# Row-wise sum of squared differences on one core: larger and uneven pieces at the end, a late piece of y, squares in place on ACT

One core of a Trainium2 chip. The metric is the device time of one execution in microseconds (us), the median of the fast runs; lower is better. The kernel is bounded by its input stream (DMA engines busy for 93.8% of the span), so a change of a few tenths of a microsecond is what there is to win, and each reading below is of that size.

## The reference

```python
batch, dim = 1024, 4096          # x and y are float32, standard normal
def reference(x, y, axis):       # axis = -1
    return np.sum((x - y) ** 2, axis=axis).astype(np.float32)
```

Two inputs of 16.8 MB each go in, 4 KB come out. Each partition holds 8 rows of 4096 columns, one after the other, so a partition reads 32768 contiguous columns of x and as many of y.

## The kernel before

Rows 0 to 3 of x and y come in one load each, rows 4 and 5 in one load each, rows 6 and 7 in eight pairs of loads that shrink towards the end. X and Y hold six rows, and rows 6 and 7 take the place of rows 0 and 1. DVE subtracts in place, ACT squares with a sum along the row, DVE squares a few small pieces itself, and the last square on DVE starts from the sum of all earlier parts of row 7 (`head`).

```python
H = 6
X = nc.alloc_sbuf_tensor("X", [P, H * D], F32).ap()
Y = nc.alloc_sbuf_tensor("Y", [P, H * D], F32).ap()
junk = nc.alloc_psum_tensor("junk", [P, D], F32).ap()

w6 = [3328, 768]
w7 = [1280, 1024, 640, 512, 320, 320]
squares = "ADAAAADD"                     # A: on ACT, D: on DVE
# ... cut ...
def square_on_act(c0, w, acc):
    h0 = c0 % (H * D)
    nc.scalar.wait_ge(diffs, n["diffs"])
    if n["acts"]:
        nc.scalar.wait_ge(acts, n["acts"])      # junk is written by all of them
    nc.scalar.activation(
        out=junk[:, 0:w], in_=X[:, h0 : h0 + w], func=Square, accum_out=acc
    ).then_inc(acts, 1)
# ... cut: rows 0 to 5; the loads of rows 6 and 7 are issued after two squares ...
for k, w in enumerate(w6 + w7):
    k7 = k - len(w6)
    if k7 == K - 1:
        add_up(head, part7)              # ahead of the last subtraction
    nc.vector.wait_ge(loaded[2 + k], 32)
    # ... cut ...
    sub(c0, w)
    # ... cut: square on ACT or DVE, the last one on DVE from head ...
```

Of the kernel before, what the change touches and what calls it, by code (L numbers as in the profile page):

```python
# [1 line left out]
_os.environ.setdefault("NEURON_RT_ULTRASERVER_MODE", "4")  # L2

# [3 lines left out]


class Program:






    def __init__(self, nc, tc):
        self.nc, self.hook = nc, tc.instruction_hook
        self.here = nc.cur_bb.bb.instructions
        self.entry = nc.main_func.blocks[0].instructions
        nc.remove_inst_callback(self.hook)  # L20
        self.lower, nc._always_lower_symbolic_ap = nc._always_lower_symbolic_ap, False
        self.before = len(self.here)

    def _take(self):
        taken = self.here[self.before :]
        del self.here[self.before :]
        return taken

    def _put(self, where):
        self.entry[where:where] = self._take()  # L30

    def early(self, engine):

        self._put(
            next(
                n
                for n, i in enumerate(self.entry)
                if i.engine == engine and str(i.opcode) == "Drain"
            )
        )  # L40

    def close(self):

        self._put(
            next(
                n for n, i in enumerate(self.entry) if str(i.opcode) == "UnconditionalBranch"
            )
        )
        self.nc._always_lower_symbolic_ap = self.lower
        self.nc.push_inst_callback(self.hook)  # L50


def kernel(tc, x, y, axis, out):
    nc = tc.nc
    P = nc.NUM_PARTITIONS
    F32 = mybir.dt.float32
    Square = mybir.ActivationFunctionType.Square
    mult, add = mybir.AluOpType.mult, mybir.AluOpType.add

    B, D = x.shape  # L60
    R = B // P


    xv = x.rearrange("(p r) d -> p (r d)", p=P)
    yv = y.rearrange("(p r) d -> p (r d)", p=P)
    ov = out.rearrange("(p r) -> p r", p=P)


    H = 6
    X = nc.alloc_sbuf_tensor("X", [P, H * D], F32).ap()  # L70
    Y = nc.alloc_sbuf_tensor("Y", [P, H * D], F32).ap()
    results = nc.alloc_sbuf_tensor("results", [P, R], F32).ap()
    junk = nc.alloc_psum_tensor("junk", [P, D], F32).ap()

    w6 = [3328, 768]
    w7 = [1280, 1024, 640, 512, 320, 320]
    squares = "ADAAAADD"
    assert sum(w6) == sum(w7) == D
    K = len(w7)
    part6 = nc.alloc_sbuf_tensor("part6", [P, len(w6)], F32).ap()  # L80
    part7 = nc.alloc_sbuf_tensor("part7", [P, K - 1], F32).ap()
    head = nc.alloc_sbuf_tensor("head", [P, 1], F32).ap()

    diffs = tc.alloc_semaphore("diffs")
    acts = tc.alloc_semaphore("acts")
    sums = tc.alloc_semaphore("sums")
    stored = tc.alloc_semaphore("stored")
    n = dict(diffs=0, acts=0, sums=0)

    prog = Program(nc, tc)  # L90

    def load(sem, src, dst, c0, c1):
        h0 = c0 % (H * D)
        nc.sync.dma_start(out=dst[:, h0 : h0 + c1 - c0], in_=src[:, c0:c1]).then_inc(sem, 16)  # L94

    loaded = []

    def load_pair(c0, c1):
        sem = tc.alloc_semaphore("loaded%d" % len(loaded))
        load(sem, xv, X, c0, c1)  # L100
        load(sem, yv, Y, c0, c1)
        loaded.append(sem)


    load_pair(0, 4 * D)
    prog.early(mybir.EngineType.SP)
    load_pair(4 * D, 6 * D)


    def sub(c0, w):  # L110
        h0 = c0 % (H * D)
        a = X[:, h0 : h0 + w]
        nc.vector.tensor_sub(out=a, in0=a, in1=Y[:, h0 : h0 + w]).then_inc(diffs, 1)  # L113
        n["diffs"] += 1

    def square_on_act(c0, w, acc):
        h0 = c0 % (H * D)
        nc.scalar.wait_ge(diffs, n["diffs"])
        if n["acts"]:
            nc.scalar.wait_ge(acts, n["acts"])  # L120
        nc.scalar.activation(  # L121
            out=junk[:, 0:w], in_=X[:, h0 : h0 + w], func=Square, accum_out=acc
        ).then_inc(acts, 1)
        n["acts"] += 1

    def square_on_dve(c0, w, acc, start):
        h0 = c0 % (H * D)
        nc.vector.wait_ge(diffs, n["diffs"])
        nc.vector.tensor_tensor_reduce(  # L129
            out=Y[:, h0 : h0 + w],  # L130
            in0=X[:, h0 : h0 + w],
            in1=X[:, h0 : h0 + w],
            scale=1.0,
            scalar=start,
            op0=mult,
            op1=add,
            accum_out=acc,
        ).then_inc(sums, 1)
        n["sums"] += 1

    def add_up(acc, parts, after=None):
        nc.vector.wait_ge(acts, n["acts"] if after is None else after)
        nc.vector.wait_ge(sums, n["sums"])  # L143
        nc.vector.tensor_reduce(  # L144
            out=acc, in_=parts, axis=mybir.AxisListType.X, op=add
        ).then_inc(sums, 1)
        n["sums"] += 1

    for r in range(6):
        if r in (0, 4):  # L150
            nc.vector.wait_ge(loaded[r // 4], 32)
        sub(r * D, D)
        square_on_act(r * D, D, results[:, r : r + 1])
        if r == 1:

            nc.sync.wait_ge(acts, 2)
            c0 = 6 * D
            for w in w6 + w7:
                load_pair(c0, c0 + w)
                c0 += w  # L160

    c0 = 6 * D
    for k, w in enumerate(w6 + w7):
        k7 = k - len(w6)
        if k7 == K - 1:
            add_up(head, part7)
        nc.vector.wait_ge(loaded[2 + k], 32)
        if k7 == K - 1:
            nc.vector.wait_ge(sums, n["sums"])  # L169
        sub(c0, w)  # L170
        if k7 < 0:
            acc = part6[:, k : k + 1]
        elif k7 < K - 1:
            acc = part7[:, k7 : k7 + 1]
        if k7 == K - 1:
            square_on_dve(c0, w, results[:, 7:8], head)
        elif squares[k] == "A":
            square_on_act(c0, w, acc)
        else:
            square_on_dve(c0, w, acc, 0.0)  # L180
        if k7 == 2:
            add_up(results[:, 6:7], part6, after=acts6)
        if k7 == -1:
            acts6 = n["acts"]
        c0 += w

    nc.sync.wait_ge(sums, n["sums"])
    nc.sync.wait_ge(acts, n["acts"])
    nc.sync.dma_start(out=ov, in_=results).then_inc(stored, 16)
    nc.sync.wait_ge(stored, 16)  # L190
    prog.close()


# [1 line left out]
_INS = ['x', 'y', 'axis']  # L195
_OUTS = [((1024,), 'float32')]

_NUMBERS = {'axis': -1}


# [26 lines left out]
```

## Time and profile before

| | before |
|---|---|
| time, median of 3 | 86.75 us |
| span of the profiled execution | 85.2 us |
| DVE busy / ACT busy | 38.0 us (45%) / 30.7 us (36%) |
| DMA engines busy | 93.8% of the span |
| last y piece landed | 81.2 |
| output store issued | 82.91 |

The page and the views behind it are shown in the prediction. In timeline lines the first number is the start in us, the second the duration; the bracket says how long the engine had been idle and what ended that. A landing is the start of a load's issue plus the time "to landing" of the list of DMA issues; that list gives it to 0.1 us, so a distance between two landings is good to about 0.1.

The profiled execution itself took 87.03 us, 0.28 more than the median of the timed runs.

### The profile page before, as it was taken

Reading aid. Unit: us, or ns where it says so; the run is one execution under the profiler, and the core shown is the slowest. Engines: PE = TensorE matmul, PEld = TensorE weight load, DVE = VectorE, ACT = ScalarE, POOL = GpSimd, SP = SyncE. Lnnn points to the kernel's source line nnn. Section 1 sums busy time; section 2 is a strip of 40 time slices with the busy share of each in tenths; the row PEclk is TensorE's granted clock in tenths of the full one; section 3 lists DMA queues with packets and bytes.
Section 4 is the critical chain, followed back from the end, with each engine's and each line's share of the span. In section 5 each row is a group of like instructions: output and inputs, shape, how many; then the busy total and the mean of one; then the engine's idle time right before and its main releaser. Section 6 shows DMA issues by size and latency. Waiting matters only on the chain.

```text
span 85.2 us, 122 instructions
## 1 busy us (share of the span) xinstructions
DVE 38.0 (45%) x22; ACT 30.7 (36%) x23; POOL 0.2 (0%) x4
## 2 busy tenths in 40 slices
DVE  0000000000000000000699999995599999997670
ACT  4100000000000000000005979797924979999800
POOL 0000000000000000000000000000000000000000
DMA  9559999997499999993899979997999999999700
GB/s 492 246 246 492 492 492 492 492 492 338 215 431 492 492 492 492 492 461 154 369 492 477 415 338 492 492 400 338 412 412 437 372 426 423 408 401 383 262 0 2
DMA packets 3024, 33.56 MB, mean 394 GB/s; under 512 B 464, under 2 KB 976, under 8 KB 2256
## 3 DMA queue, kind: packets, MB, share of 16 engines
q1 hardware_dynamic: 3024, 33.56, 93.8%
HBM read 33.55 MB, written 0.00 MB: 394 GB/s over the span
## 4 chain that ended last, share of the span: by engine, by line
DMA 63%; SPq 15%; DVE 13%; ACT 4%; issue 1%; DVEq 0%
DMA Y<-in_y_dram 63%; SPq L94 15%; DVE X L113 11%; ACT junk L121 4%; DVE Y L129 1%; DVE head L144 0%; DVEq L169 0%; DVEq L143 0%; DVE part L129 0%; DVEq L222 0%
## 5 line engine op out<-in xcount | busy, mean ns | idle before, releaser
L113 DVE TENSOR_TENSOR X<-X,Y 128x4096 f32<-128x4096 f32 (+7 forms) x14 | 35.8, 2594 | 44.7 <-DMA Y<-in_y_dram 44.6
L121 ACT ACTIVATE junk<-X 128x4096 f32<-128x4096 f32 (+5 forms) x11 | 28.1, 2550 | 49.0 <-DVE X L113 48.6
L121 ACT ACTIVATION_READ_ACCUMULATOR junk<-X 128x1 f32 x11 | 2.0, 186 | 0.0
L121 ACT ACT_TABLE_LOAD x1 | 1.3, 1283 | 1.3 <-PEq L208 1.3
L129 DVE CUSTOM_DVE_ANT_0 Y<-X 128x768 f32<-128x768 f32 (+1 forms) x2 | 1.4, 724 | 0.1
L129 DVE CUSTOM_DVE_ANT_0 Y<-X,head 128x320 f32<-128x320 f32 x1 | 0.6, 552 | 0.0
L144 DVE TENSOR_REDUCE head<-part 128x1 f32<-128x5 f32 x1 | 0.2, 158 | 0.1
L129 DVE DVE_READ_ACCUMULATOR2_ANT part<- 128x1 f32 x2 | 0.2, 82 | 0.0
L144 DVE TENSOR_REDUCE results<-part 128x1 f32<-128x2 f32 x1 | 0.1, 150 | 0.0
L208 POOL MEMSET const-bfloat16-1.0<- 128x1 bf16 x1 | 0.1, 101 | 0.0
L208 POOL MEMSET const-uint8-127<- 128x1 uint8 x1 | 0.1, 101 | 0.0
L208 POOL MEMSET const-float32-0.0<- 128x1 f32 x1 | 0.1, 98 | 0.2 <-issue 0.2
L208 POOL MEMSET const-float32-1.0<- 128x1 f32 x1 | 0.1, 98 | 0.0
L129 DVE DVE_READ_ACCUMULATOR2_ANT results<- 128x1 f32 x1 | 0.1, 83 | 0.0
## 6 DMA issues: line engine op xcount, KB each, us to landing
X<-in_x_dram SPq DMA_DIRECT2D x1, 4096.0 KB, 49.7
Y<-in_y_dram SPq DMA_DIRECT2D x1, 4096.0 KB, 59.0
X<-in_x_dram SPq DMA_DIRECT2D x1, 1664.0 KB, 10.9
Y<-in_y_dram SPq DMA_DIRECT2D x1, 1664.0 KB, 14.6
X<-in_x_dram SPq DMA_DIRECT2D x1, 640.0 KB, 16.7
Y<-in_y_dram SPq DMA_DIRECT2D x1, 640.0 KB, 17.8
X<-in_x_dram SPq DMA_DIRECT2D x1, 512.0 KB, 18.6
Y<-in_y_dram SPq DMA_DIRECT2D x1, 512.0 KB, 19.4
```

What stands on the lines that cost most here:

```text
L94: nc.sync.dma_start(out=dst[:, h0 : h0 + c1 - c0], in_=src[:, c0:c1]).then_inc(sem, 16)
L113: nc.vector.tensor_sub(out=a, in0=a, in1=Y[:, h0 : h0 + w]).then_inc(diffs, 1)
L121: nc.scalar.activation(out=junk[:, 0:w], in_=X[:, h0 : h0 + w], func=Square, accum_out=acc).then_inc(acts, 1)
L129: nc.vector.tensor_tensor_reduce(out=Y[:, h0 : h0 + w], in0=X[:, h0 : h0 + w], in1=X[:, h0 : h0 + w], scale=1.0, scalar=start, op0=mult, o ...
L144: nc.vector.tensor_reduce(out=acc, in_=parts, axis=mybir.AxisListType.X, op=add).then_inc(sums, 1)
L208: nc = _bacc.Bacc("TRN2", target_bir_lowering=False, num_devices=1)
```

## The change

Its intent is to lose less at the end of the stream: fewer and larger pieces, none of DVE's time for squares except the very last, and, between the last large piece and the final pair, a piece of y that needs no x beside it (736 columns of row 3, left out of the first y load). The loads of the first 3072 columns of row 6 are issued one square earlier. Squares are written over the differences in X, so ACT no longer waits for its own previous square.

```diff
-    w6 = [3328, 768]
-    w7 = [1280, 1024, 640, 512, 320, 320]
-    squares = "ADAAAADD"
+    xw = [16384, 8192, 3072, 2688, 1312, 768, 352]
+    yw = [15648, 8192, 3072, 2688, 1312, 768]
+    late, last = 736, 352
+    LATE = 3
+    cut = (LATE + 1) * D - late
 ...
+    ys += [(cut, cut + late), (N - last, N)]      # y order: ..., late piece, last piece
 ...
-        if n["acts"]:
-            nc.scalar.wait_ge(acts, n["acts"])
-        nc.scalar.activation(
-            out=junk[:, 0:w], in_=X[:, h0 : h0 + w], func=Square, accum_out=acc
-        ).then_inc(acts, 1)
+        nc.scalar.activation(out=a, in_=a, func=Square, accum_out=acc).then_inc(acts, 1)
 ...
+            if tail:                               # row 3 = its first part + the late part
+                nc.scalar.wait_ge(acts, n["acts"])
+                nc.scalar.activation(
+                    out=results[:, r : r + 1], in_=b, func=Identity, bias=a
+                ).then_inc(acts, 1)
+            if r in (0, 1):                        # the 3072 columns of row 6 after one square, the rest after two
+                nc.sync.wait_ge(acts, n["acts"])
 ...
+            if final:                              # sub, then head, then the last square
+                nc.vector.tensor_reduce(out=head, in_=parts_of(r, len(row_parts[r]) - 1), ...)
+                nc.vector.tensor_tensor_reduce(..., scalar=head, accum_out=results[:, r : r + 1])
```

The 2688 columns span the end of row 6 (1024) and the start of row 7 (1664).

More of the change, by code (lines that the diff above doesn't have):

```diff
@@ L57 @@
     Square = mybir.ActivationFunctionType.Square
+    Identity = mybir.ActivationFunctionType.Identity
     mult, add = mybir.AluOpType.mult, mybir.AluOpType.add
@@ L61 @@
     R = B // P
+    N = R * D
     xv = x.rearrange("(p r) d -> p (r d)", p=P)
@@ L66 @@
     ov = out.rearrange("(p r) -> p r", p=P)
-    H = 6
-    X = nc.alloc_sbuf_tensor("X", [P, H * D], F32).ap()
-    Y = nc.alloc_sbuf_tensor("Y", [P, H * D], F32).ap()
+    H = 6 * D
+    X = nc.alloc_sbuf_tensor("X", [P, H], F32).ap()
+    Y = nc.alloc_sbuf_tensor("Y", [P, H], F32).ap()
     results = nc.alloc_sbuf_tensor("results", [P, R], F32).ap()
-    junk = nc.alloc_psum_tensor("junk", [P, D], F32).ap()
-    w6 = [3328, 768]
-    w7 = [1280, 1024, 640, 512, 320, 320]
-    squares = "ADAAAADD"
-    assert sum(w6) == sum(w7) == D
-    K = len(w7)
-    part6 = nc.alloc_sbuf_tensor("part6", [P, len(w6)], F32).ap()
-    part7 = nc.alloc_sbuf_tensor("part7", [P, K - 1], F32).ap()
-    head = nc.alloc_sbuf_tensor("head", [P, 1], F32).ap()
+    xw = [16384, 8192, 3072, 2688, 1312, 768, 352]
[3 more added lines that the diff above has]
+    cut = (LATE + 1) * D - late
+    assert sum(xw) == N and sum(yw) == N - late - last
+    xs, c = [], 0
+    for w in xw:
+        xs.append((c, c + w))
+        c += w
+    ys, c = [], 0
+    for w in yw:
+        ys.append((c, c + w))
+        c += w
+        if c == cut:
+            c += late
+    ys += [(cut, cut + late), (N - last, N)]
     diffs = tc.alloc_semaphore("diffs")
@@ L90, with home @@
     prog = Program(nc, tc)
-    def load(sem, src, dst, c0, c1):
-        h0 = c0 % (H * D)
-        nc.sync.dma_start(out=dst[:, h0 : h0 + c1 - c0], in_=src[:, c0:c1]).then_inc(sem, 16)
-    loaded = []
-    def load_pair(c0, c1):
-        sem = tc.alloc_semaphore("loaded%d" % len(loaded))
-        load(sem, xv, X, c0, c1)
-        load(sem, yv, Y, c0, c1)
-        loaded.append(sem)
-    load_pair(0, 4 * D)
-    prog.early(mybir.EngineType.SP)
-    load_pair(4 * D, 6 * D)
-    def sub(c0, w):
-        h0 = c0 % (H * D)
-        a = X[:, h0 : h0 + w]
-        nc.vector.tensor_sub(out=a, in0=a, in1=Y[:, h0 : h0 + w]).then_inc(diffs, 1)
+    def home(c0, c1):
+        h0 = c0 % H
+        return slice(h0, h0 + c1 - c0)
@@ new lines, with load @@
+    landed_x, landed_y = [], []
+    freed = []
+    def load(landed, src, dst, name, c0, c1):
+        sem = tc.alloc_semaphore("%s%d" % (name, len(landed)))
+        nc.sync.dma_start(out=dst[:, home(c0, c1)], in_=src[:, c0:c1]).then_inc(sem, 16)
+        landed.append(((c0, c1), sem))
+    order = []
+    have = 0
+    for c0, c1 in ys:
+        while have < c1:
+            order.append((landed_x, xv, X, "x") + xs[len([o for o in order if o[3] == "x"])])
+            have = order[-1][5]
+        order.append((landed_y, yv, Y, "y", c0, c1))
@@ new lines @@
+    todo = list(order)
+    for _ in range(2):
+        load(*todo.pop(0))
+    prog.early(mybir.EngineType.SP)
+    while todo and todo[0][5] <= H:
+        load(*todo.pop(0))
+    row_parts = [[] for _ in range(R)]
+    for c0, c1 in ys:
+        while c0 < c1:
+            e = min(c1, (c0 // D + 1) * D)
+            row_parts[c0 // D].append((c0, e))
+            c0 = e
+    parts, where = None, {}
+    total = sum(len(p) for p in row_parts if len(p) > 1)
+    parts = nc.alloc_sbuf_tensor("parts", [P, total], F32).ap()
@@ new lines, with parts_of, wait_loaded @@
+    head = nc.alloc_sbuf_tensor("head", [P, 1], F32).ap()
+    k = 0
+    for r, p in enumerate(row_parts):
+        for piece in p:
+            where[piece] = parts[:, k : k + 1] if len(p) > 1 else results[:, r : r + 1]
+            k += len(p) > 1
+    first = {}
+    k = 0
+    for r, p in enumerate(row_parts):
+        if len(p) > 1:
+            first[r] = k
+            k += len(p)
+    def parts_of(r, m):
+        return parts[:, first[r] : first[r] + m]
+    seen_x = [0]
+    def wait_loaded(c1, ysem):
+        waits = []
+        while seen_x[0] < len(xs) and xs[seen_x[0]][0] < c1:
+            waits.append(seen_x[0])
+            seen_x[0] += 1
+        nc.vector.wait_ge(ysem, 16)
+        for k in waits:
+            nc.vector.wait_ge(landed_x[k][1], 16)
@@ L114, in sub, with square @@
+    def sub(c0, c1):
+        a = X[:, home(c0, c1)]
+        nc.vector.tensor_sub(out=a, in0=a, in1=Y[:, home(c0, c1)]).then_inc(diffs, 1)
         n["diffs"] += 1
-    def square_on_act(c0, w, acc):
-        h0 = c0 % (H * D)
+    def square(c0, c1, acc):
+        a = X[:, home(c0, c1)]
         nc.scalar.wait_ge(diffs, n["diffs"])
-        if n["acts"]:
-            nc.scalar.wait_ge(acts, n["acts"])
-        nc.scalar.activation(
-            out=junk[:, 0:w], in_=X[:, h0 : h0 + w], func=Square, accum_out=acc
-        ).then_inc(acts, 1)
-        n["acts"] += 1
@@ L126, in square_on_dve @@
-    def square_on_dve(c0, w, acc, start):
-        h0 = c0 % (H * D)
-        nc.vector.wait_ge(diffs, n["diffs"])
-        nc.vector.tensor_tensor_reduce(
-            out=Y[:, h0 : h0 + w],
-            in0=X[:, h0 : h0 + w],
-            in1=X[:, h0 : h0 + w],
-            scale=1.0,
-            scalar=start,
-            op0=mult,
-            op1=add,
-            accum_out=acc,
-        ).then_inc(sums, 1)
-        n["sums"] += 1
-    def add_up(acc, parts, after=None):
-        nc.vector.wait_ge(acts, n["acts"] if after is None else after)
-        nc.vector.wait_ge(sums, n["sums"])
-        nc.vector.tensor_reduce(
-            out=acc, in_=parts, axis=mybir.AxisListType.X, op=add
-        ).then_inc(sums, 1)
-        n["sums"] += 1
@@ L149 @@
-    for r in range(6):
-        if r in (0, 4):
-            nc.vector.wait_ge(loaded[r // 4], 32)
-        sub(r * D, D)
-        square_on_act(r * D, D, results[:, r : r + 1])
-        if r == 1:
-            nc.sync.wait_ge(acts, 2)
-            c0 = 6 * D
-            for w in w6 + w7:
-                load_pair(c0, c0 + w)
-                c0 += w
-    c0 = 6 * D
-    for k, w in enumerate(w6 + w7):
-        k7 = k - len(w6)
-        if k7 == K - 1:
-            add_up(head, part7)
-        nc.vector.wait_ge(loaded[2 + k], 32)
-        if k7 == K - 1:
-            nc.vector.wait_ge(sums, n["sums"])
-        sub(c0, w)
-        if k7 < 0:
-            acc = part6[:, k : k + 1]
-        elif k7 < K - 1:
-            acc = part7[:, k7 : k7 + 1]
-        if k7 == K - 1:
-            square_on_dve(c0, w, results[:, 7:8], head)
-        elif squares[k] == "A":
-            square_on_act(c0, w, acc)
-        else:
-            square_on_dve(c0, w, acc, 0.0)
-        if k7 == 2:
-            add_up(results[:, 6:7], part6, after=acts6)
-        if k7 == -1:
-            acts6 = n["acts"]
-        c0 += w
+        nc.scalar.activation(out=a, in_=a, func=Square, accum_out=acc).then_inc(acts, 1)
@@ new lines, in square @@
+        n["acts"] += 1
+    squared = {}
+    reuse = []
+    for j, (c0, c1) in enumerate(ys):
+        final, tail = j == len(ys) - 1, j == len(ys) - 2
+        wait_loaded(c1, landed_y[j][1])
+        pieces = []
+        while c0 < c1:
+            e = min(c1, (c0 // D + 1) * D)
+            pieces.append((c0, e))
+            c0 = e
+        for piece in pieces:
+            sub(*piece)
+            r = piece[0] // D
+            if final:
+                nc.vector.wait_ge(acts, squared[row_parts[r][-2]])
+                nc.vector.tensor_reduce(
+                    out=head, in_=parts_of(r, len(row_parts[r]) - 1), axis=mybir.AxisListType.X, op=add
+                ).then_inc(sums, 1)
+                n["sums"] += 1
+                nc.vector.wait_ge(sums, n["sums"])
+                nc.vector.wait_ge(diffs, n["diffs"])
+                nc.vector.tensor_tensor_reduce(
+                    out=Y[:, home(*piece)],
+                    in0=X[:, home(*piece)],
+                    in1=X[:, home(*piece)],
+                    scale=1.0,
+                    scalar=head,
+                    op0=mult,
+                    op1=add,
+                    accum_out=results[:, r : r + 1],
+                ).then_inc(sums, 1)
+                n["sums"] += 1
+                continue
+            square(*piece, where[piece])
+            squared[piece] = n["acts"]
+            if tail:
+                a, b = parts_of(r, 1), parts[:, first[r] + 1 : first[r] + 2]
+                nc.scalar.wait_ge(acts, n["acts"])
+                nc.scalar.activation(
+                    out=results[:, r : r + 1], in_=b, func=Identity, bias=a
+                ).then_inc(acts, 1)
+                n["acts"] += 1
+            if r in (0, 1):
+                nc.sync.wait_ge(acts, n["acts"])
+                while todo and todo[0][5] <= H + (r + 1) * D:
+                    load(*todo.pop(0))
+                if r == 1:
+                    while todo:
+                        load(*todo.pop(0))
+        if j == len(ys) - 4:
+            r = 6
+            nc.vector.wait_ge(acts, squared[row_parts[r][-1]])
+            nc.vector.tensor_reduce(
+                out=results[:, r : r + 1],
+                in_=parts_of(r, len(row_parts[r])),
+                axis=mybir.AxisListType.X,
+                op=add,
+            ).then_inc(sums, 1)
+            n["sums"] += 1
```

## The prediction

> **What bounds the kernel now.** I read the page's busy shares and its DMA row first, then the list of DMA issues, then the timeline of the last microseconds, and the chain of waits last.
>
> ```profile
> span 85.2 us, 122 instructions
> DVE 38.0 (45%) x22; ACT 30.7 (36%) x23; POOL 0.2 (0%) x4
> DMA  9559999997499999993899979997999999999700
> q1 hardware_dynamic: 3024, 33.56, 93.8%
> ```
>
> Both compute engines are idle for more than half of the span, while the 16 DMA engines are busy almost from the first slice to slice 38, that is to about 80.5 us. The kernel is one stream of 33.56 MB, and work before it starts and after it ends. So a change can win only in four places: the start, gaps in the stream, the cost of cutting the stream into pieces, and the drain after the last bytes.
>
> The list of DMA issues gives the time from issue to landing; with the start of each issue from the timeline it gives landings.
>
> ```profile
> Y<-in_y_dram SPq DMA_DIRECT2D x1, 4096.0 KB, 59.0
> X<-in_x_dram SPq DMA_DIRECT2D x1, 21.9
> Y<-in_y_dram SPq DMA_DIRECT2D x1, 40.8
> ```
>
> The first x load (rows 0 to 3, 8.389 MB), issued at 0.00, landed at 21.9; the first y load, issued at 0.43, at 41.2. The second took 19.3 us for 8.389 MB: 434 GB/s is the full rate, and the first paid 2.6 us more, the start-up. The y load of rows 4 and 5, issued at 1.64, landed at 60.64. The rest (16 loads, rows 6 and 7) was issued from 53.77 on, 7 us before the queue would have run dry, so there is no gap.
>
> The end of the stream, from the timeline and from the issues of the stretch 70.5 to 86 us:
>
> ```profile
> 79.47 0.69 DVE L113 TENSOR_TENSOR X<-X,Y 128x512 f32<-128x512 f32 x1 [0.47 <-DMA Y<-in_y_dram]
> 80.40 0.49 DVE L113 TENSOR_TENSOR X<-X,Y 128x320 f32<-128x320 f32 x1 [0.23 <-DMA Y<-in_y_dram]
> 80.93 0.49 DVE L129 CUSTOM_DVE_ANT_0 Y<-X 128x320 f32<-128x320 f32 x1
> ...
> 81.53 0.16 DVE L144 TENSOR_REDUCE head<-part 128x1 f32<-128x5 f32 x1
> 81.80 0.49 DVE L113 TENSOR_TENSOR X<-X,Y 128x320 f32<-128x320 f32 x1
> 82.32 0.55 DVE L129 CUSTOM_DVE_ANT_0 Y<-X,head 128x320 f32<-128x320 f32 x1
> 82.80 0.08 DVE L129 DVE_READ_ACCUMULATOR2_ANT results<- 128x1 f32 x1
> 82.91 0.35 SPq L189 DMA_DIRECT2D out_dram<-results  x1
> ...
> Y<-in_y_dram SPq DMA_DIRECT2D x1, 160.0 KB, 9.6
> ```
>
> The last y piece was issued at 71.61 and landed 9.56 us later (the two 160 KB y loads average 11.4, and the other took 13.24 in the chain), at 81.17. But the last subtraction began only at 81.80: DVE was still squaring and adding up for the piece before. So the end today is 81.17 of stream, 0.63 of a busy DVE, 1.11 of last subtraction and square (81.80 to 82.91), and 2.29 from the output store to the end of the span.
>
> The chain of waits agrees on the last part, but its largest shares must be read with care:
>
> ```profile
> DMA 63%; SPq 15%; DVE 13%; ACT 4%; issue 1%; DVEq 0%
> ```
>
> The 15% of SPq are the issues between 53.77 and 67.14, some lasting 3 us [...]. DMA engines were busy all that time, so shortening them buys nothing.
>
> [...] the new cuts at columns 15648, 31648 and 32416 start 128 B off (31648 x 4 B = 494.5 x 256). [...] The squares now go to SBUF in place; I allow 0 to 40 ns each.
>
> **The change, part by part.**
>
> *Fewer, larger pieces.* After the y load of rows 4 and 5, before took 81.17 - 60.64 = 20.53 us for 8.389 MB; at 434 GB/s that is 19.33. The excess of 1.20 over 16 loads is 0.075 us per load. The new kernel has 11 loads there: x and y of 3072, 2688, 1312, 768 and 352, and the 736 columns of y row 3. Those are 0.377 MB and come out of the first y load, so rows 4 and 5 land 0.87 earlier, at 59.77. Then 8.766 MB / 434 = 20.20, plus 11 x 0.075 = 0.83: the last y lands at 80.79. Saved: 5 x 0.075 = 0.38. Against that, five loads start 128 B off. [...] 80.9 for the last landing.
>
> *Earlier issue of row 6.* Its loads now wait for the square of row 0 alone, at about 48.5 instead of 53.8. The stream was full anyway: 0.
>
> *The late piece of row 3.* It needs no x load, so it puts 0.94 us of transfer (0.87 + 0.075) between the last large piece and the final pair, in which DVE and ACT catch up. Landings by the same sum: y3072 67.2, y2688 73.7, y1312 76.9, y768 78.9, late 79.8 [...], final 80.8 to 81.0. [...] rows 4 and 5 until 68.5, 3072 until 71.9, then 1024 and 1664 of the 2688 from 73.7 to 76.7, 1312 from 76.9 to 78.45, the reduce of row 6, 768 from 78.9 to 79.9, 736 until 80.8. So DVE is just free when the final pair lands. That removes the 0.63 of busy DVE.
>
> *Squares on ACT.* This removes two DVE squares (958 and 491 ns; only the second was on the path, inside the 0.63 above) and adds ACT work late. The wait of ACT for its own previous square goes, because nothing writes the same junk any more; it showed as about 0.08 us between the accumulator read and the next ACTIVATE. ACT: 1664 from 76.75, 1312 from 78.5, 768 from about 80.0, 736 from 80.9 to 81.9 with its read (186 ns). Then a wait of about 0.08, and the Identity that adds row 3, about 0.28: done at 82.2 to 82.4. If Identity needed another table load (1283 ns here) it would be 83.6, but the build shows one load only.
>
> *The end of the chain.* The add-up into head now stands between the final subtraction and the final square: 81.53 to 81.80 was 0.27 for that step. 32 more columns in two instructions cost 2 x 32 / 0.96 = 0.07. So the store is issued at the landing + 0.02 + 1.11 + 0.27 + 0.07 = landing + 1.47 = 82.37. Before had 1.74 after the landing.
>
> *Sum.* Landing 81.17 to 80.9: -0.27. Drain 1.74 to 1.47: -0.27. Together -0.54 by DVE; by ACT's Identity, at up to 82.4, it is -0.5. The span should be about 84.7, and the time 86.75 - 0.54 = **86.2**.
>
> **Rivals.** *ACT becomes the end.* DVE and ACT finish within 0.2 us of each other in my sum. If squares in place are 40 ns longer, or ACT queues behind the 3072 and 1664 pieces, Identity ends at 82.6 to 82.8: time 86.45 to 86.65. The profile speaks for it (ACT has no idle time in the last slices of before and gets more to do), and against it: pieces of 1312, 768 and 736 cost ACT 1.27, 0.83 and 0.80, no more than their transfers bring in.
>
> *The cuts off 256 B cost more than the pieces save.* Then the stream ends at 81.1 or later, and only the drain gains: 86.5. For it, the 320-column loads already run at 360 to 370 GB/s in the last slices of before, so small rows are not free. [...]
>
> *A clean finish.* If the cost per load sits mainly in the smallest loads (320 and 512 columns, of which before had six) and the misalignment costs nothing, the last y lands at 80.5 and the store goes out at 82.0, with ACT also 0.2 earlier: 85.8.
>
> *Nothing moves.* If the stream has a floor that the pieces don't set, only the drain's 0.27 is left: again about 86.5.
>
> **Range and chances.** The rivals span 85.8 to 86.65, and runs of before differ by 0.06. I take 85.8 to 86.6. Faster by over 2% means under 85.0, or 1.7 us. Even all of the cutting cost (1.20) and half a microsecond of drain would be needed, and 11 cuts remain: 3%. Slower by over 2% would need a stream that breaks or a late table load of more than 1.3 us: 2%.
>
> **What would show it.** Right: the last y lands 0.2 to 0.4 us earlier than 81.17, the final 352 subtraction starts on a DMA wait and not behind other DVE work, the store goes out near 82.4, and fewer packets (about 2160) fill the same 33.56 MB. Wrong: the final subtraction starts behind the 736 one; or the store is released by ACT's Identity well after DVE's last read; or the last landing doesn't move. A result outside the range would most likely mean that the cost per load is not 0.075.

With all terms the sum came to -0.54, and 86.2. The cuts take out what stood behind one of them: the step of the last landing from 80.79 to 80.9, the author's estimate of 0.1 for the five loads that start 128 B off (half of what was feared, hence "80.8 to 81.0"). Without it the terms worked out from the trace come to 0.38 + 0.27 = 0.65, and 86.1.

The durations that the working uses can be had from the trace of before. Subtractions took 4422 ns for 4096 columns and 492 for 320, so 1.04 ns per further column: the 0.96 columns per ns of the last step, and the line on which DVE's times from "rows 4 and 5 until 68.5" to "736 until 80.8" lie. Squares on ACT took 3588 ns for 4096 columns and 1028 for 1024, so 0.83 per further column; 1312, 768 and 736 columns were put at 1.27, 0.83 and 0.80 us and took 1.30, 0.83 and 0.82 in the trace of after. The Identity, put at 0.28, took 0.29 there. Both pages list one ACT_TABLE_LOAD, of 1283 ns. What a write into X costs beside one into PSUM was not known: "0 to 40 ns" was the guess (29 ns by the two traces, 3617 beside 3588 for 4096 columns).

## The result

The changed kernel takes 85.94 us (four runs, 85.87 to 86.17) beside 86.75: a ratio of 0.9908, with a 95% interval of 0.9885 to 0.993. Ratios are the mean time of one kernel's fast runs over that of the other's of the same rounds, so not quite the ratio of the medians quoted here. The interval lies wholly below 1. A second measurement on another chip gave 86.03 beside 86.93, a ratio of 0.9893. The gain of 0.8 to 0.9 us lies inside the predicted range, and is more than the 0.55 that was expected.

The page after, the lines that answer to those shown of before:

```profile
span 84.1 us, 110 instructions
DVE 36.3 (43%) x17; ACT 31.6 (38%) x26; POOL 0.2 (0%) x4
q1 hardware_dynamic: 2304, 33.56, 94.1%
DMA 71%; DVE 14%; ACT 10%; SPq 1%; issue 0%
```

The same bytes in fewer packets, and still a stream that fills the span. The 15% of SPq in the chain of waits is gone. The prediction put their worth at nothing, as the DMA engines were busy beside them (a share of 0.99 from 53.77 to 70.40 us in before, `--windows`); the gain is accounted for below without them, but no run tried them by themselves.

The end, from the timeline after:

```profile
78.23 1.30 ACT L178 ACTIVATE X<-X 128x1312 f32<-128x1312 f32 x1
78.52 2.34 DVE L172 TENSOR_TENSOR X<-X,Y 128x768 f32<-128x768 f32 x3 [0.26 <-DMA Y<-in_y_dram]
79.43 0.19 ACT L178 ACTIVATION_READ_ACCUMULATOR X<-X 128x1 f32 x1
79.53 0.83 ACT L178 ACTIVATE X<-X 128x768 f32<-128x768 f32 x1
80.26 0.19 ACT L178 ACTIVATION_READ_ACCUMULATOR X<-X 128x1 f32 x1
80.39 0.82 ACT L178 ACTIVATE X<-X 128x736 f32<-128x736 f32 x1
80.77 0.15 DVE L196 TENSOR_REDUCE head<-parts 128x1 f32<-128x3 f32 x1
81.00 0.58 DVE L202 CUSTOM_DVE_ANT_0 Y<-X,head 128x352 f32<-128x352 f32 x1
81.11 0.18 ACT L178 ACTIVATION_READ_ACCUMULATOR X<-X 128x1 f32 x1
81.33 0.29 ACT L219 ACTIVATE results<-parts 128x1 f32<-128x1 f32 x1
81.52 0.08 DVE L202 DVE_READ_ACCUMULATOR2_ANT results<- 128x1 f32 x1
81.71 0.35 SPq L245 DMA_DIRECT2D out_dram<-results  x1
```

And the last loads in its list of DMA issues (the last y was issued at 61.30):

```profile
Y<-in_y_dram SPq DMA_DIRECT2D x1, 4096.0 KB, 58.0
...
Y<-in_y_dram SPq DMA_DIRECT2D x1, 176.0 KB, 19.0
```

Three subtractions (768, 736, 352) stand in one merged line, x3: they run back to back, the last from 80.3 to 80.86. The last y landed at 61.30 + 19.0 = 80.3, so DVE was free just when it came: between "on a DMA wait" and "behind the 736 one", the two signs that the prediction named, this is a tie. DVE ends at 81.60 (81.52 + 0.08), ACT's Identity at 81.62 (81.33 + 0.29): a tie as well. The store goes out at 81.71. ACT has no pause in these lines: the profile's chain (`--critical --window 78:85`) follows the end back through ACT's squares without a break to 76.56. So two paths end together, one from the last landing through DVE and one from the 2688 columns through ACT.

From landing to store it is 1.41, where before it was 1.70 (82.91 - 81.21). So of the gain, 0.3 is drain, and the rest came from an earlier end of the stream, which the prediction had put at 0.27.

### The profile page after: what moved, and what is told of

The parts are those of the page before. It is cut to its first block, busy times and chain, and to the rows that moved or that the text cites. A ratio compares the mean times of both kernels' runs of the same rounds, so it can differ in the third digit from the quotient of the medians.

```text
span 84.1 us, 110 instructions
## 1 busy us (share of the span) xinstructions
DVE 36.3 (43%) x17; ACT 31.6 (38%) x26; POOL 0.2 (0%) x4
## 2 busy tenths in 40 slices
DMA packets 2304, 33.56 MB, mean 399 GB/s; under 512 B 384, under 2 KB 640, under 8 KB 1280
## 3 DMA queue, kind: packets, MB, share of 16 engines
q1 hardware_dynamic: 2304, 33.56, 94.1%
## 4 chain that ended last, share of the span: by engine, by line
DMA 71%; DVE 14%; ACT 10%; SPq 1%; issue 0%
DMA Y<-in_y_dram 71%; DVE X L172 14%; ACT X L178 10%; SPq L114 1%; ACT results L219 0%
## 5 line engine op out<-in xcount | busy, mean ns | idle before, releaser
L172 DVE TENSOR_TENSOR X<-X,Y 128x4096 f32<-128x4096 f32 (+8 forms) x13 | 35.6, 2781 | 45.2 <-DMA Y<-in_y_dram 45.1
L178 ACT ACTIVATE X<-X 128x4096 f32<-128x4096 f32 (+7 forms) x12 | 29.4, 2449 | 48.7 <-DVE X L172 48.7
L178 ACT ACTIVATION_READ_ACCUMULATOR X<-X 128x1 f32 x12 | 2.2, 186 | 0.0
L178 ACT ACT_TABLE_LOAD x1 | 1.3, 1283 | 1.3 <-PEq L264 1.3
L202 DVE CUSTOM_DVE_ANT_0 Y<-X,head 128x352 f32<-128x352 f32 x1 | 0.6, 583 | 0.1
```

What stands on the lines that cost most here:

```text
L172: nc.vector.tensor_sub(out=a, in0=a, in1=Y[:, home(c0, c1)]).then_inc(diffs, 1)
L178: nc.scalar.activation(out=a, in_=a, func=Square, accum_out=acc).then_inc(acts, 1)
L202: nc.vector.tensor_tensor_reduce(out=Y[:, home(*piece)], in0=X[:, home(*piece)], in1=X[:, home(*piece)], scale=1.0, scalar=head, op0=mult, ...
```

## The experiments

"Before" beside a time is the kernel before in the same rounds on the same chip. All outputs are right.

### before_again: the kernel before, for a second trace

> The kernel before, unchanged, for a second trace. The first trace came from an execution of 87.03 us, 0.28 above the median of 86.75, and the prediction took its landing of 81.17 from it. If that execution was slow in the stream, this one shows a span near 84.9 and the last y landing near 80.9, with the same 1.7 us from landing to store. If the landing is again near 81.17, the stream of the changed kernel really ends 0.87 earlier, and the cost per load was mis-sized. Time 86.75.

Measured: 86.97 beside 86.93, ratio 0.9998 (0.9981 to 1.0016): two copies of one kernel agree. The trace is of an execution of 86.73, with a span of 84.9.

```profile
Y<-in_y_dram SPq DMA_DIRECT2D x1, 160.0 KB, 9.6
...
82.60 0.35 SPq L189 DMA_DIRECT2D out_dram<-results  x1
```

The last y, issued at 71.28, landed at 80.88; the store followed 1.72 later. This execution was the fastest of its six (median 86.97), and the first one was 0.28 over its median. So the first trace was late in the stream, by 0.3 at most, and the drain is the same in both. Executions of one kernel differ by as much as the terms in question, and landings should be compared as distances from an earlier landing: from the y of rows 4 and 5 to the last y, 20.57 and 20.36 in the two traces of before.

### after_again: the changed kernel, as base

> The changed kernel, unchanged, as the base for the others on this chip and for a second trace. Time 85.9 to 86.0, last y landing 80.3 within 0.1 if the traced execution was typical, 80.5 to 80.7 if it was a lucky one.

Measured: 86.03 beside 86.93. Last landing 80.47 (61.47 + 19.0), store at 81.88, again 1.41 later. From the y of rows 4 and 5 to the last y it is 20.64, and 20.66 in the first trace of after, although 0.377 MB more pass in it than in before (0.87 us at 434 GB/s, the rate of the second load in the first trace of before). The landing is 0.17 later than in the first trace, just short of what was expected if that one had been lucky; this execution was at its median, the first (85.87) 0.07 under it.

### no_late: without the late piece

```diff
-    yw = [15648, 8192, 3072, 2688, 1312, 768]
-    late, last = 736, 352
+    yw = [16384, 8192, 3072, 2688, 1312, 768]
+    late, last = 0, 352
-    ys += [(cut, cut + late), (N - last, N)]
+    ys += [(N - last, N)]
 # ... cut: the skip over the late piece and the Identity go, one index follows ...
```

> The changed kernel without the late piece of row 3: y is cut like x, and the Identity goes. Theory 1 (the late piece gives ACT and DVE time to finish the 768 columns behind it): the 768 pair lands some 0.9 us later, near 79.4, its square on ACT ends near 81.35 with its read, the add-up into head waits for it, and the store goes out near 82.2: time 86.4 to 86.5. Rival (the gain is in the stream alone, and the late piece is one load more): the time falls by 0.04 to 0.08, to 85.85.

Measured: 86.45 beside 86.93, 0.42 slower than the changed kernel. Its timeline has the wait that the late piece avoids:

```profile
80.52 0.84 ACT L176 ACTIVATE X<-X 128x768 f32<-128x768 f32 x1
81.27 0.19 ACT L176 ACTIVATION_READ_ACCUMULATOR X<-X 128x1 f32 x1
81.49 0.16 DVE L194 TENSOR_REDUCE head<-parts 128x1 f32<-128x3 f32 x1 [0.54 <-ACT X L176]
```

The last y lands at 80.44, about as in the base. But the square of the 768 columns comes 0.8 later (80.52, and 79.71 in after_again), and DVE idles 0.54 for it before it can add up. Theory 1 holds; the late piece is worth about 0.4 us in this kernel, all of it in the drain (1.86 from landing to store, against 1.41).

### junk_psum: squares into scratch, with the wait for the previous one

```diff
+    junk = nc.alloc_psum_tensor("junk", [P, D], F32).ap()
 ...
-        nc.scalar.activation(out=a, in_=a, func=Square, accum_out=acc).then_inc(acts, 1)
+        if n["acts"]:
+            nc.scalar.wait_ge(acts, n["acts"])
+        nc.scalar.activation(out=junk[:, 0 : c1 - c0], in_=a, func=Square, accum_out=acc).then_inc(acts, 1)
```

> The changed kernel with the squares written to the PSUM scratch again and each ACTIVATE waiting for the one before, as in the kernel before. In the trace of the changed kernel an ACTIVATE starts 0.09 before the end of the accumulator read ahead of it, in before 0.09 after it: 0.18 us per square. If that is on the path, ACT's chain of 1312, 768, 736 and Identity ends 0.35 to 0.5 later and the store is released by it: 86.35 to 86.5. If ACT has slack: 86.0 to 86.1.

Measured: 86.40 beside 86.95, a gain over before of 0.55 where the base has 0.90. In the trace ACT's Identity ends at 82.18 and the store goes out at 82.27, while DVE was done at 81.71:

```profile
81.63 0.08 DVE L205 DVE_READ_ACCUMULATOR2_ANT results<- 128x1 f32 x1
81.66 0.19 ACT L181 ACTIVATION_READ_ACCUMULATOR junk<-X 128x1 f32 x1
81.88 0.30 ACT L222 ACTIVATE results<-parts 128x1 f32<-128x1 f32 x1
82.27 0.35 SPq L248 DMA_DIRECT2D out_dram<-results  x1
```

ACT is on the path at the end, so what it saves per square counts. The lines after show it: the read ahead of the 768 runs from 79.43 to 79.62 and the ACTIVATE starts at 79.53, 0.09 before its end; in before the next ACTIVATE started 0.09 after the end of the read (77.81 and 77.90):

```profile
77.62 0.19 ACT L121 ACTIVATION_READ_ACCUMULATOR junk<-X 128x1 f32 x1
77.90 1.03 ACT L121 ACTIVATE junk<-X 128x1024 f32<-128x1024 f32 x1
```

The run takes wait and destination together, and none separates them. By the traces the wait is the larger part: the durations differ by little, and the other way round (3617 ns in place, 3588 ns into PSUM, for 4096 columns).

### before_acts: all squares but the last on ACT, in the kernel before

```diff
-    squares = "ADAAAADD"
+    squares = "AAAAAAAD"
```

> The kernel before with one part of the change alone: the squares of the 768 and of the first 320 columns go from DVE to ACT, so ACT has all squares except the last; scratch in PSUM, own wait, cuts and order stay. By the trace of before, ACT is busy without a break from 73.28 on; a 768 there (0.82 + 0.25) pushes everything behind it back by about 1.0, the 320 on ACT ends near 82.5, the add-up into head waits for it and the store goes out near 83.9: time 87.8 to 88.0. The reading in the prediction (the move takes 0.63 of DVE work off the end and ACT only just keeps up) would give 86.3 to 87.0 if it held without the late piece and the squares in place.

Measured: 87.97 beside 87.00, ratio 1.0117 (1.0085 to 1.0149). The move of the squares by itself costs a microsecond:

```profile
82.19 0.19 ACT L121 ACTIVATION_READ_ACCUMULATOR junk<-X 128x1 f32 x1
82.40 0.16 DVE L144 TENSOR_REDUCE head<-part 128x1 f32<-128x5 f32 x1 [1.74 <-ACT junk L121]
```

DVE waits 1.74 us for ACT's backlog. In the changed kernel the same assignment does not hold up the end: fewer squares stand behind each other, they do not wait for one another, and there is the late piece. Whether the move gains anything there is not shown, as no run puts squares back on DVE in the changed kernel. Parts of a change are not always a sum.

### aligned: every cut on a multiple of 256 B of the input

```diff
-    xw = [16384, 8192, 3072, 2688, 1312, 768, 352]
-    yw = [15648, 8192, 3072, 2688, 1312, 768]
-    late, last = 736, 352
+    xw = [16384, 8192, 3072, 2688, 1344, 768, 320]
+    yw = [15680, 8192, 3072, 2688, 1344, 768]
+    late, last = 704, 320
```

> The changed kernel with every cut at a multiple of 64 columns, that is of 256 B (y row 3 at 15680, row 7 at 31680 and 32448; pieces 1344, 704 and 320 for 1312, 736 and 352). [...] If the start does not matter: only the 0.07, about 85.85.

Measured: 86.29 beside 86.93, slower than the base by 0.26, although its last pieces are smaller. The theory that stands above missed (about 85.85). So did the one that is cut, an estimate that no run showed, by which starts that are off cost time and this kernel takes 85.65 to 85.7. Both missed in the same direction. The pair of 768 columns took 1.96 us from landing to landing (77.03 to 78.99), in the base 1.80 (76.85 to 78.65). The columns are the same, only the start differs. So cuts that are *off* a multiple of 256 B looked faster.

### cut12 and cut12_off: the same question, made large

The loads of the 3072 columns of row 6 are cut in 12; the subtraction stays one and waits for all. In cut12 each piece has 256 columns; in cut12_off the first has 288 and the last 224.

```diff
+        pieces = 12 if c1 - c0 == 3072 else 1
+        w = (c1 - c0) // pieces
+        for i in range(pieces):
+            o = 32 if pieces > 1 else 0            # cut12: o = 0
+            a = c0 + i * w + (o if i else 0)
+            b = c0 + (i + 1) * w + (o if i < pieces - 1 else 0)
+            nc.sync.dma_start(out=dst[:, home(a, b)], in_=src[:, a:b]).then_inc(sem, 16)
```

> The changed kernel with the loads of the 3072 columns of row 6 cut into 12 of 256 columns each (1 KB per partition, every start on a multiple of 256 B), the subtraction still one: 22 loads more, far ahead of the end. If a load costs 0.075 whatever its size, the end comes 1.65 later: 87.65. If it costs what the changed kernel's tail shows, about 0.045: 1.0 later, 87.0. If the cost were paid only in the last loads before the end, nothing: 86.0.

> As cut12, but the first piece is 288 columns and the last 224, so the 11 starts between lie 128 B off a multiple of 256 B in the input and in the tile. [...] If starts that are off make the loads faster, as the slow run of the aligned cuts hints (0.12 us for a pair of 768 columns): over 1 us faster than cut12. If the start does not matter: the same as cut12.

Measured: cut12 88.25 (87.81 to 88.83), cut12_off 87.11 (87.06 to 87.13), before 86.95. Off is 1.14 faster, as the theory that starts off make the loads faster had it. (cut12 itself is slower than even the dearest of its theories, 87.65, and its runs spread by 1.0, so against before it is unclear by the 2% rule.) Each row below is the stretch 60 to 66 us, in which only these pieces pass: stretch, length, busy DVE and ACT and POOL with the number of instructions, granted clock, DMA share, GB/s; cut12 first.

```profile
60.00:66.00 6.00, 6.00 (x2) 1.86 (x3) 0.00 (x0) 1.00 1.10 360
```

```profile
60.00:66.00 6.00, 6.00 (x2) 1.89 (x3) 0.00 (x0) 1.00 1.09 380
```

The DMA share is full in both, so the queue never ran empty; the same engines moved less per microsecond. And the cost of a load is no matter of the end alone: 22 loads more, 12 us ahead of the last landing, put off the end (the subtraction that waits for all of them starts at 70.07 in cut12 and 69.08 in cut12_off; the last y lands at 82.34 and 81.30).

### before_off128: ten loads of the kernel before, 128 B off

```diff
-    w7 = [1280, 1024, 640, 512, 320, 320]
+    w7 = [1312, 1024, 640, 512, 320, 288]
```

> The kernel before with row 7 cut 32 columns later (1312, 1024, 640, 512, 320, 288 for 1280, 1024, 640, 512, 320, 320): ten loads now start 128 B off. The last DVE work shrinks by 32 columns in two instructions, 0.07 us. If the start does not matter: 86.85, beside 86.93 of before on the last chip. [...] If off starts help by 0.06 per load: the last landing 0.6 earlier and the time near 86.3.

Measured: 86.50 beside 86.95, ratio 0.9963 (0.9942 to 0.9985): 0.45 faster by the medians, of which 0.07 is the smaller last piece. Its traced execution was its slowest (87.01), but it lost its time early: the y of rows 4 and 5 landed only at 61.03. From there to the last y it is 20.15, 0.2 to 0.4 less than in the two traces of before, for ten loads moved.

### The address on the other side, and cut12_pad, before_pad, aligned_pad

That the inputs start on multiples of 256 B is assumed here; no view shows it. (Were they 128 B off, yes and no would change places in the column of reads below, and the comparison would stay.) But where do the tiles start? The memory map of the build has X at byte 16512 of a partition and Y at 114816: both 128 over a multiple of 256. So every cut at a multiple of 64 columns reads from a multiple of 256 B and writes to an address 128 B off, and a cut 32 columns beside it does the reverse. The three runs above can't tell the two sides apart. One unused tile of 128 B ahead of X can: it moves X to 16640 and Y to 114944, and the small tiles behind them by the same 128 B.

```diff
+    pad = nc.alloc_sbuf_tensor("pad", [P, 32], F32).ap()
     X = nc.alloc_sbuf_tensor("X", ...)
```

> As cut12 (88.25 beside 86.95 of before), with one tile of 32 columns that nothing uses allocated ahead of X. The build puts X at byte 16512 and Y at 114816 of a partition, 128 over a multiple of 256, so a cut at a multiple of 64 columns reads from a multiple of 256 B and writes to an address 128 off; cut12_off did the reverse (87.11). With the tile, X is at 16640 and Y at 114944, and the 12 pieces are on multiples on both sides. Theory (the write address decides, the read address does not): the 22 added loads and the large ones gain 0.05 each, the five small ones that are now off on the write side lose it: 86.7 to 87.1. Rival (the read address decides, off is better): the same as cut12, 88.2.

> The kernel before with that one unused tile: all 20 loads now write to multiples of 256 B, nothing else changes. Theory: 20 x 0.05 = 1.0 us off the last landing: 85.9 to 86.1 beside 86.93. If only the cut12 pieces or only small rows care, 86.5 at best; if the read address decides, 86.93.

> The cuts of aligned (86.29 beside 86.93) with the unused tile: all 15 loads read from and write to multiples of 256 B. Theory: 15 x 0.05 = 0.75 less than aligned: 85.5 to 85.7, faster than the changed kernel (86.03) and than before. Rival (read address): 86.29, as aligned.

| kernel | reads start at a multiple of 256 B | writes start at one | time | before |
|---|---|---|---|---|
| cut12 (its 12 pieces) | yes | no | 88.25 | 86.95 |
| cut12_off (11 of 12) | no | yes | 87.11 | 86.95 |
| cut12_pad (its 12 pieces) | yes | yes | 87.11 | 86.91 |
| aligned | yes | no | 86.29 | 86.93 |
| aligned_pad | yes | yes | 85.99 | 86.91 |
| before_pad | yes | yes | 86.43 | 86.91 |

The write address decides, and the start of the read shows no cost: with the pieces' writes on multiples, 87.11 and 87.11, whether the reads are or not. (Pieces off on both sides were not run, and the two kernels differ in a few other loads; the landings below are the cleaner measure.) In the kernel before, the unused tile alone saves 0.48 us (ratio 0.9953, 0.9931 to 0.9975).

How much per load? These are the lines of y2688, the y load of the 2688 columns, in cut12 (issued at 64.81), cut12_off (64.76) and cut12_pad (64.63):

```profile
Y<-in_y_dram SPq DMA_DIRECT2D x1, 1344.0 KB, 10.7
Y<-in_y_dram SPq DMA_DIRECT2D x1, 1344.0 KB, 9.7
Y<-in_y_dram SPq DMA_DIRECT2D x1, 1344.0 KB, 9.7
```

From the landing of the y of rows 4 and 5 to that of y2688 it is 15.67 in cut12, 14.74 in cut12_off (22 loads moved onto multiples) and 14.61 in cut12_pad (26 loads): 0.93 / 22 and 1.06 / 26 are both about 0.041 us a load (each from one trace). Without the extra cuts it is 13.73 with writes on multiples (aligned_pad), and 13.84 and 13.87 with writes off (the two traces of after; the same loads take 13.86 in no_late, 13.89 in junk_psum, 14.02 in aligned). So a further load of 1 KB rows costs (14.61 - 13.73) / 22 = 0.040 when it writes to multiples of 256 B, and (15.67 - 13.85) / 22 = 0.083 when it doesn't. The prediction had taken 0.075 for all.

The expectations for before_pad (85.9 to 86.1) and aligned_pad (85.5 to 85.7) overshot: they put 0.05 on each of 20 and 15 loads (1.14 / 22, from the times of cut12 and cut12_off). The gains were 0.48 and 0.30. The landings say where the rest went. From the y of rows 4 and 5 to the last y, before_pad takes 19.99, 0.4 to 0.6 less than the two traces of before, for 16 loads: 0.02 to 0.04 each. aligned_pad takes 20.52 and aligned 20.98: 0.46 for 11 loads, 0.042 each. The four large loads ahead of that show no gain (the y of rows 4 and 5 landed at 59.84 and 59.72, one trace each). And in aligned_pad a part is lost in the drain:

```profile
81.51 0.30 ACT L220 ACTIVATE results<-parts 128x1 f32<-128x1 f32 x1
81.57 0.08 DVE L203 DVE_READ_ACCUMULATOR2_ANT results<- 128x1 f32 x1
81.89 0.35 SPq L246 DMA_DIRECT2D out_dram<-results  x1
```

The last y landed at 80.36. DVE was done at 81.65, but ACT's Identity ended at 81.81 and held the store until 1.53 after the landing. In aligned ACT was last too (82.01, DVE 81.90), but the store followed the landing by 1.41. So a faster stream now runs into ACT. aligned_pad gains 0.92 on before and the changed kernel 0.90, on different chips: no version that clearly beats both was found.

## Why the prediction was right, and where it was off

**The bound** was read right. The stream fills the span before and after, in both traces of the changed kernel the last subtraction starts within 0.05 of the last landing, and no part of the gain has to be put down to the vanished share of the DMA-issuing queue.

**The drain** was right in mechanism and size: 1.74 to 1.47 was predicted, and 1.70 to 1.41 is what the traces show. The add-up moved behind the last subtraction, and DVE came free just as the last pair landed. That the late piece does this is shown by no_late: 0.42 of the gain is lost without it.

**ACT and DVE within 0.2 us at the end** was right: 81.62 and 81.60. The reason given was partly too small: dropping ACT's wait was put at 0.08 per square, and the traces show 0.18. Without this, and with squares into PSUM again, ACT is the end by about half a microsecond (junk_psum). The rival in which ACT becomes the end is therefore what happens as soon as this saving is taken away; the step from SBUF instead of PSUM was 29 ns for 4096 columns, inside the 0 to 40 allowed.

**The stream** was right in direction and wrong in size, and this is where the missing 0.3 us lies. The step was "Against that, five loads start 128 B off", for which 0.1 was charged (an estimate that no run shows), together with 0.075 for each of the 11 loads. It looked at the input's addresses and not at the tile's. In the tile, the five loads that start 128 B off in the input (both of 768, the 736, both of 352) are the only ones in either kernel whose writes start on a multiple of 256 B. By cut12 and cut12_pad such a load costs 0.040 and not 0.075, which saves about 0.2, where 0.1 was charged. These loads themselves agree: from y2688 to the last y the two traces of after take 6.79 and 6.80, and aligned, which moves the five loads off and has 0.04 less to transfer, takes 6.96, so 0.20 for five loads. The predicted gain of 0.27 in the stream becomes some 0.57; the measured 0.81 and 0.90 less 0.3 of drain leave 0.5 to 0.6. In the prediction's own terms, 0.83 for the 11 loads and 0.1 for the odd cuts were added to the 20.20 of their bytes; both traces show 0.45 in their place (20.65).

So a part of what seemed to come from larger pieces came from odd cuts that happened to match an odd tile address. That part was luck. Without it the kernel gains 0.64 (aligned, 86.29 beside 86.93), of which 0.07 is its smaller last piece; 0.55 was predicted. With it, two of the prediction's own signs missed: the last y landed at 80.30 and 80.47, 0.7 to 0.9 ahead of 81.17 where 0.2 to 0.4 was forecast, and the store went out at 81.71 and 81.88, not near 82.4.

**The penalty** was put on the wrong side: the prediction charged 0.1 for five starts off in the input, which show no cost (87.11 and 87.11), and none for the writes, where a start off costs 0.041 per load.

**Also off:** the packet count (2160 predicted, 2304 found) because 14 loads were counted instead of 15: 15 x 128 rows, 128 for the output, and 16 for each of 16 DMAs make 2304, and the same count makes the 3024 of before (20 x 128 + 128 + 16 x 21). And the working took its landing of 81.17 from an execution that was late by up to 0.3, which a second trace showed; the drain, read as a difference, didn't suffer from it. For ACT's path the working sets the end of the Identity equal to the store; the trace has 0.09 between them (81.62 and 81.71).

**What stays open:** why a write that starts off a multiple of 256 B costs this much, and how its cost depends on the length of the rows and on the start itself (every start tried lay on a multiple of 256 B or 128 B off one). The early issue of row 6, the smaller number of pieces and the squares on ACT were not tried by themselves in either direction, except that before_acts puts the squares on ACT in the kernel before. The removals (0.42 for the late piece, 0.35 for the squares in place, 0.26 for the odd cuts) sum to more than the gain, and before_acts alone loses 1.0: these are the losses if one part is taken out of this kernel, not shares of 0.9.

## What to carry to other kernels

When a stream is the bound, count what each further load costs (here 0.040 or 0.083 us per load of 128 rows of 1 KB), and look up where the tiles start in memory before choosing cuts: here an unused tile of 128 B per partition was worth 0.5 us without any other change. At the end of a stream, put a transfer that the last dependent sum doesn't need between the last large piece and the final one, so that the engines are free when the final one lands: here that was worth 0.42 us. Before moving work to the less busy engine, look whether it has time in the last microseconds. The busy share over the span doesn't say so: ACT's was 36% in the kernel before, and there the move made DVE wait 1.74 us for it and cost a microsecond.
